# A hybrid encoder step on one NeuronCore: RWKV-7's triangular inverse on TensorE instead of GpSimd, and all queues in the order of a list scheduler

## The chip, the core and the metric

The kernel runs on one core of one Trainium2 chip. The metric is the device time of one execution in microseconds (us), the median of several runs. A core has TensorE (PE; its weight loads are shown as PEld), VectorE (DVE), ScalarE (ACT), GpSimd (POOL) and SyncE (SP, which here only issues DMA transfers). Each works through a queue of its own, in order; semaphores make one wait for another. The program fixes the order of every queue when it is built.

## The reference, cut to what matters

One inference step of a two-layer encoder trunk, in float32, for a prompt of 512 tokens and a sample of 32 tokens with states of its own. Layer 0: half SwiGLU, a mixer of RG-LRU and retention, cross-attention to a memory, half SwiGLU. Layer 1 the same with RWKV-7 as its mixer. Each part ends in `x = LayerNorm(ALPHA * x + part(x))`. The RWKV-7 recurrence, for each of 16 heads with 64 keys and 64 values, is

```
def step(S, inp):
    r_t, w_t, k_t, v_t, kk_t, b_t = inp
    sa = jnp.einsum('bhvk,bhk->bhv', S, -kk_t)
    S = S * w_t[:, :, None, :] + sa[..., None] * b_t[:, :, None, :] + v_t[..., None] * k_t[:, :, None, :]
    return S, jnp.einsum('bhvk,bhk->bhv', S, r_t)
...
s_last, o = lax.scan(step, s0.astype(f32), (tm(r), tm(decay), tm(k), tm(v), tm(kk), tm(kk * iclr)))
```

Done by chunks of 32 tokens it needs, for every chunk and head, the inverse of a triangular 32x32 matrix I + N with ones on the diagonal, where N (strictly triangular) holds the products of the chunk's keys among each other.

## The kernel before, in words

*The halves.* All 544 tokens lie as columns: half A has 256 columns, half B 288 (256 of the prompt and the sample's 32). Features lie on partitions. Two Python generators (`half_main`, one per half) walk through the eight stages of `STAGES`; a small task runner (`Kern.run`) switches between them and side tasks, and so decides in which order instructions are emitted.

*Products with weights.* `linear` takes a granule, a block of 128 columns of weights and up to 1024 rows: 512 KB, loaded by SyncE's queue to a buffer `wr`, split into a high and a low part in a slot `W` (ScalarE writes the high part, VectorE or GpSimd subtracts for the low part, `_split`), and multiplied in 24 matmuls of 128x128 by 256 or 288 columns: high by high, low by high, high by low. Usually both halves share a granule. Between layer 1's mixer and its end each half loads its own (`SOLO`), so that one half's products can fill the other's waits; half A may run ahead to the end there, but only behind its own recurrence.

*The recurrence (stage mix1).* `wkv` borrows three weight slots, one load buffer, two of the four PSUM banks of the products and three of the other four. It goes over nine blocks: four of 64 tokens of A, four of B and the sample's 32; a block has one or two chunks of 32 tokens. Five tasks run side by side, coupled by events:

- `wkv_prep` makes the decays, keys and rows of a block; its first instruction is a product on GpSimd (`K.gtt(a4, k, vb("k_k"))`, line 1807). For each chunk it multiplies the keys (KL) by the rows (X) into the masked 32x32 matrices, and writes N to DRAM (`dn`, line 1861). Event `kl` marks a chunk, `kb` the block.
- `wkv_solve` (lines 1873 to 1912) waits for `kb`. It loads N back with a head, chunk and quarter of the rows to a partition (tile P, line 1886), clears Z (in tile LC), and runs 31 steps of forward substitution on GpSimd, two operations each. Z goes to DRAM (`dz`) and from there in four loads into the corners of block-diagonal 128x128 matrices (`tb`, in a slot W; two buffers, so a block waits for the chain of the second block before it). Then it fires `prep`.
- `wkv_load` transposes keys and values for a chunk.
- `wkv_chain` is the recurrence itself, chunk after chunk: 16 products X by state (96 rows to 32 columns of the array), one eviction, four products with the inverse (128x128, line 1986), four evictions, 16 products that update the state, four VectorE operations, and 16 products for the output.
- `wkv_norm` norms a block's output and applies the gate.

*The order of the work.* Every instruction goes through `plan`, which asks `Clock.op` when it would run by an estimate (an engine's occupied times and its operands' times; tasks of a negative band, the recurrence among them, are planned as if other work were not there). The estimate becomes the instruction's priority (`cur_priority`, line 386), and the tile framework's own scheduler (`schedule_with_timeline_sim=True`, line 2083) puts the queues in order by these priorities and its own simulated times.

Of the kernel before, what the change touches and what calls it, by code (L numbers as in the profile page):

```python
# [3 lines left out]

# [42 lines left out]
MEM_FILL = 28  # L47
LOG_G = np.log1p(-(2.0 ** (-5.0 - np.arange(4, dtype=np.float32)))).astype(np.float32)
# [3 lines left out]
def const_arrays():  # L52
# [32 lines left out]
    c["wmask"] = m  # L85
    sg = np.ones((128, 1), np.float32)
# [16 lines left out]
class Res:  # L103
    """Things that are taken and given back, with the times from which they are free."""
# [27 lines left out]
class Line:  # L132
    """The spans of time in which an engine is taken; a later comer may fill a gap."""
# [28 lines left out]
class Clock:  # L162
    """An estimate of when instructions run, in ns: what an engine does and what its operands wait for.
    It orders the emission and the engines' queues, and nothing else rests on it."""
# [24 lines left out]
    def ready(self, outs, ins=()):  # L189
        """When the operands of a transfer are free and written."""  # L190
# [9 lines left out]
    def renew(self, old, new):  # L200
        """A tile takes over the room of an older one."""
        if old is not None and old.tensor.name in self.cells:
            c = self.area(new)[0]
            c[1] = self.cells.pop(old.tensor.name).max()
# [43 lines left out]

class Arena:
# [26 lines left out]
    def top(self, n):  # L276
        """The last n elements."""
# [50 lines left out]
class Arenas:  # L328
    """Several arenas as one."""
# [44 lines left out]
class Kern(Clock):  # L374
    def __init__(self, tc, ins, outs, consts, stages):
        super().__init__()
        self.tc, self.nc, self.i, self.o, self.c = tc, tc.nc, ins, outs, consts
# [6 lines left out]
    def plan(self, eng, dur, outs, ins, queue=None):  # L384
        s = self.op(eng, dur, outs, [t for t in ins if t is not None and not isinstance(t, (int, float))], self.band, queue)
        self.tc.cur_priority = 10000000 + int(s) + self.band * (BAND if self.band > 0 else 0000)

    def mm(self, out, lhsT, rhs, start=True, stop=True):
        n = free_size(rhs)
        if lhsT.dtype == F32R:  # L390
            cost = (n if n >= 256 else max(4 * n, 128)) / 2.4 + 2
        else:
            cost = 4 * (max(n, 62) / 2.4) + 2
        self.plan("pe", cost, [out], [lhsT, rhs])
        self.nc.tensor.matmul(out, lhsT, rhs, start=start, stop=stop)  # L395

    def tr(self, out, in_, k0=0):
        k = in_.shape[0]
        self.plan("pe", 109.0, [out], [in_])
        self.nc.tensor.transpose(out, in_, self.ident[k0:k0 + k, k0:k0 + k])  # L400

    def _v(self, out, ins, fast=False):
        fast = fast and all(t.space != PSUM for t in ins)
# [1684 lines left out]
```

## Time and profile before

| | |
|---|---|
| median of 3 runs | 3021.44 us (3020.57 to 3023.3) |
| span of the profiled execution | 3028.7 us |
| instructions | 54637 |
| PE / PEld / DVE / ACT / POOL busy | 2833.4 / 2716.3 / 1743.4 / 1276.8 / 830.1 us |
| HBM read | 313.09 MB, 108 GB/s over the span with the writes |
| mean granted TensorE clock | 0.945 |

The span is what the profiler saw between the first and the last instruction of one execution; nothing else of that execution's time is recorded. In the rows of the profile a name such as `mm<-XHB,W` means: PSUM tile mm written from tiles XHB and W; a line is that of a helper (395 is every matmul, 408 a VectorE product, 412 a GpSimd product, 486 a ScalarE activation, 491 a DMA), so one goes by tiles. A float32 matmul has two entries in the trace, a float32r matmul one. Busy time of PE counts every matmul from its start to its modelled end, so the tail of a lone matmul counts as busy. The granted clock is 1.00 at full speed.

### The profile page before, as it was taken

The page shows a single profiled execution, that of the slowest core. Times are in us where ns is not written, and L with a number is a line of the kernel's source. Part 1 is how long each engine was busy: PE and PEld are TensorE (multiplying, and loading weights), DVE is VectorE, ACT ScalarE, POOL GpSimd, SP SyncE. Part 2 cuts the span into 40 slices and gives each one's busy share as a digit, 9 for nine tenths or more (in the row PEclk, how much of TensorE's full clock was granted, in tenths as well). Part 3 has the DMA queues.
Part 4 walks back from the last instruction along what each step waited for, and adds up shares of the span by engine and source line. Part 5 has one row for each costly group of instructions (what it writes and reads, how often), then busy time and mean ns, then how long its engine had stood idle before and what let it go on. Part 6 is the DMA issues. An engine that isn't in the chain of part 4 may idle for free.

```text
span 3028.7 us, 54637 instructions
## 1 busy us (share of the span) xinstructions
PE 2833.4 (94%) x22456; PEld 2716.3 (90%) x22456; DVE 1743.4 (58%) x3099; ACT 1276.8 (42%) x2184; POOL 830.1 (27%) x1088
## 2 busy tenths in 40 slices
PE   9999998998999999999999898888878889999998
PEld 8999998998998999989999897776767779998997
DVE  5333337677767333365355756674675666767655
ACT  4223233665545222234244343343435455655544
POOL 2001104333313000032011212466375543422301
PEclk9999999999999999999999998788778879999999
DMA  6443443322332232322356453122223135645563
GB/s 182 126 119 115 130 119 97 88 68 81 98 98 84 85 90 84 89 87 77 90 155 179 120 168 106 39 65 62 69 73 87 49 98 174 177 141 157 169 176 93
DMA packets 626331, 330.56 MB, mean 109 GB/s; under 512 B 45480, under 2 KB 620160, under 8 KB 626080
## 3 DMA queue, kind: packets, MB, share of 16 engines
q1 hardware_dynamic: 617952, 317.06, 36.8%
q0 software_dynamic: 3488, 9.44, 1.0%
q8 instruction: 176, 2.88, 0.4%
q10 hardware_dynamic: 4640, 0.56, 0.1%
q14 instruction: 75, 0.61, 0.1%
HBM read 313.09 MB, written 13.92 MB: 108 GB/s over the span
## 4 chain that ended last, share of the span: by engine, by line
PE 66%; DVE 10%; POOL 9%; DMA 7%; ACT 5%; issue 3%; SPq 0%; ACTq 0%; DVEq 0%; POOLq 0%
PE mm L395 60%; PE ax L395 4%; POOL LC L412 3%; POOL P L412 3%; DMA P<-dn 3%; DVE W L408 2%; ACT arena L486 1%; ACT W L486 1%; DVE arena L408 1%; DMA wr<-in_ffn_up 1%; PE ax L400 1%; DVE arena L432 1%; POOL arena L412 1%; ACT L2049 1%; DVE XB L408 1%
## 5 line engine op out<-in xcount | busy, mean ns | idle before, releaser
L486 ACT ACTIVATE W<-wr 128x1024 fp32r<-128x1024 f32 (+1 forms) x558 | 577.0, 1038 | 737.4 <-PE mm L395 560.0
L408 DVE TENSOR_TENSOR W<-wr,W 128x1024 fp32r<-128x1024 f32 (+1 forms) x455 | 561.5, 1236 | 551.7 <-ACT W L486 542.8
L395 PE MATMUL mm<-XHB,W 128*128 128x288 f32 x3840 | 585.1, 302 | 14.1 <-ACT XHB L486 4.7
L395 PE MATMUL mm<-XHA,W 128*128 128x256 f32 x3840 | 538.4, 290 | 28.9 <-ACT XHA L486 11.6
L395 PEld LDWEIGHTS mm<-XHB,W 128*128 128x128 f32 x3840 | 532.4, 191 | 25.0 <-ACT XHB L486 5.8
L395 PEld LDWEIGHTS mm<-XHA,W 128*128 128x128 f32 x3840 | 499.7, 194 | 39.7 <-ACT XHA L486 16.0
L412 POOL TENSOR_TENSOR W<-wr,W 128x1024 fp32r<-128x1024 f32 (+1 forms) x103 | 251.0, 2439 | 606.2 <-ACT W L486 550.6
L395 PE MATMUL mm<-XLB,W 128*128 128x288 f32 x1984 | 318.7, 300 | 0.7 <-DVE XLB L408 0.7
L395 PE MATMUL mm<-HHB,W 128*128 128x288 f32 x1920 | 291.0, 301 | 11.4 <-ACT W L486 4.4
L395 PEld LDWEIGHTS mm<-XLB,W 128*128 128x128 f32 x1984 | 283.0, 190 | 3.2 <-DVE XLB L408 1.1
L395 PE MATMUL mm<-XLA,W 128*128 128x256 f32 x1984 | 284.7, 283 | 0.0
L395 PEld LDWEIGHTS mm<-HHB,W 128*128 128x128 f32 x1920 | 267.0, 191 | 15.0 <-ACT W L486 5.3
L395 PE MATMUL mm<-HHA,W 128*128 128x256 f32 x1920 | 265.7, 288 | 5.9 <-POOL W L412 2.2
L395 PEld LDWEIGHTS mm<-XLA,W 128*128 128x128 f32 x1984 | 259.1, 190 | 0.3 <-DVE XLA L408 0.2
L395 PEld LDWEIGHTS mm<-HHA,W 128*128 128x128 f32 x1920 | 247.1, 192 | 8.8 <-POOL W L412 2.6
L486 ACT ACTIVATE arena<-mm 128x256 f32<-128x256 f32 (+4 forms) x292 | 112.2, 387 | 305.1 <-PE mm L395 287.5
L432 DVE SCALAR_TENSOR_TENSOR arena<-mm,arena 128x288 f32<-128x288 f32 (+1 forms) x176 | 77.2, 439 | 157.7 <-PE mm L395 149.0
L395 PE MATMUL mm<-HLB,W 128*128 128x288 f32 x896 | 144.3, 301 | 0.3 <-DVE HLB L408 0.3
L412 POOL TENSOR_TENSOR P<-LC,P 128x66 f32<-128x66 f32 (+24 forms) x279 | 113.5, 407 | 84.6 <-DMA P<-dn 64.6
L395 PEld LDWEIGHTS mm<-HLB,W 128*128 128x128 f32 x896 | 130.1, 193 | 0.6 <-DVE HLB L408 0.5
L395 PE MATMUL mm<-HLA,W 128*128 128x256 f32 x896 | 129.3, 284 | 0.0
L412 POOL TENSOR_TENSOR LC<-LC,P 128x66 f32<-128x66 f32 (+24 forms) x279 | 115.0, 412 | 20.5
(426 smaller groups left out, 3612.0 us busy)
## 6 DMA issues: line engine op xcount, KB each, us to landing
wr<-in_ffn_up SPq DMA_DIRECT2D x246, 512.0 KB
wr<-in_ffn_down SPq DMA_DIRECT2D x96, 448.0 KB
wr<-in_l_w_rkv SPq DMA_DIRECT2D x48, 512.0 KB
wr<-in_ffn_down SPq DMA_DIRECT2D x40, 512.0 KB
wr<-in_l_w_in SPq DMA_DIRECT2D x24, 512.0 KB
wr<-in_l_w_out SPq DMA_DIRECT2D x24, 512.0 KB
wr<-in_xa_q SPq DMA_DIRECT2D x24, 512.0 KB
wr<-in_xa_o SPq DMA_DIRECT2D x24, 512.0 KB
```

Of the source, the lines that this page charges most:

```text
L395: self.nc.tensor.matmul(out, lhsT, rhs, start=start, stop=stop)
L400: self.nc.tensor.transpose(out, in_, self.ident[k0:k0 + k, k0:k0 + k])
L408: self.nc.vector.tensor_tensor(out, a, b, op=op)
L412: self.nc.gpsimd.tensor_tensor(out, a, b, op=op)
L432: self.nc.vector.scalar_tensor_tensor(out, a, s, b, op0=op0, op1=op1)
L486: return self.nc.scalar.activation(out, a, f, bias=bias, scale=scale, **kw)
L2049: nc.scalar.preload_act_table_set(name)
```

## The change

Two things change. First, `wkv_solve` computes the inverse on TensorE. For a chunk and group of four heads, four 32x32 matrices lie one below the other on 128 partitions; `product` multiplies them pairwise, each with a 32x32 corner of the array of its own (rows 32q, columns 32q). N comes straight from the keys and rows by 16 products per chunk, in both orientations. Masks (a new constant `winv` in tile LC) cut it into a block diagonal of 8x8 blocks and two bands outside; (I + D)^-1 of the diagonal comes from three doublings, and two steps widen it to 16 and to 32. There are no DRAM copies any more (`dn` and `dz` go), `tb` holds only the 32x32 matrices and has three buffers, and the chain's product by the inverse is 16 matmuls of 32x32 instead of 4 of 128x128. The evictions go to VectorE and ScalarE, one small sum to GpSimd. The solve's PSUM banks are those of the preparation. In the preparation the gates' products take one bank after the other instead of two at once, and seven products may go to GpSimd (`ett` instead of `tt`, and `f` for the first of two halves).

```
+    c["winv"] = np.tile(inv, (4, 1, 1))
...
     for b, (h, t0, L) in enumerate(w.blk):
         nch = L // 32
...
-        yield lambda: b < 2 or event(K, "chain", b - 2).set
...
-        for s in range(31):
-            nr, nt = s // 4 + 1, 31 - s
-            T = w.t[:, :nr * nt].rearrange("p (i t) -> p i t", i=nr)
-            K.gtt(T, Z[:, :nr, s:s + 1].to_broadcast([128, nr, nt]),
-                  N[:, s:s + 1, s + 1:].to_broadcast([128, nr, nt]))
-            K.gtt(Z[:, :nr, s + 1:], Z[:, :nr, s + 1:], T, ALU.subtract)
...
+        yield lambda: b < 3 or event(K, "chain", b - 3).set
...
+        def product(out, left, right):
+            for g in range(4 * nch):
+                for q in range(4):
+                    u = slice(32 * q, 32 * q + 32)
+                    K.mm(out[u, g], left[u, g], right[u, g], side=4)
...
+        ps, up, lo = yield from bank()
+        for c in range(nch):
+            X, KL = w.ck[b, c][:2]
+            for hd in range(16):
+                g, q = divmod(hd, 4)
+                u = slice(32 * q, 32 * q + 32)
+                K.mm(up[u, 4 * c + g], KL[0:64, hd, 32:64], X[0:64, hd, 32:64], side=4)
...
+        K.tt(dt, up, m(0))
+        K.tt(d, lo, m(1))
+        K.tt(et, up, m(2))
+        K.tt(ft, up, m(3))
+        w.ps.give(ps)
+        K.gtt(idt, dt, m(4), ALU.add)
+        yield
+        ps, p, pt = yield from bank()
+        product(p, dt, d)
+        product(pt, d, dt)
...
+        K.act(d2, both)
+        K.tt(id2, p, m(4), ALU.add)
...
+        product(p, d2[:, 1], d2[:, 0])
+        product(pt, id2, idt)
+        K.tt(id4, p, m(4), ALU.add)
+        K.act(gt, pt)
...
+        product(p, gt, id4)
+        product(pt, id4, gt)
...
+        K.act(t8, both)
...
+        product(p, et, t8[:, 0])
+        K.tt(iw, m(4), p, ALU.subtract)
...
+        product(p, t8[:, 1], iw)
+        product(pt, iw, t8[:, 1])
...
+        K.act(t16, both)
...
+        product(p, ft, t16[:, 0])
+        K.tt(iw2, m(4), p, ALU.subtract)
...
+        product(p, iw2, t16[:, 1])
+        K.act(cut(w.tb[b % 3]), p)
...
-            K.mm(pu[:, g * 64:g * 64 + 64], TB[:, 4 * c + g], RS[:, g])
+            for q in range(4):
+                u = slice(32 * q, 32 * q + 32)
+                K.mm(pu[u, g * 64:g * 64 + 64], TB[u, 4 * c + g], RS[u, g], side=4)
```

Second, the program is built twice. In the first pass a `Graph` notes every instruction with its engine, a price, its operands' dependencies and its planned start as a priority. `Graph.schedule` then runs a list scheduler over the whole graph: at each moment an engine takes, among the instructions whose operands are ready, the one with the earliest planned start. ScalarE may prefer one that needs no change of its function table (up to `SWAP` ns of priority), VectorE's operations on SBUF and GpSimd exclude each other, and transfers share one line. In the second pass `chain` ties each engine's instructions together in the order of these start times, and the framework's own simulation is off. The prices of `plan` change with it: a fixed 147 ns for VectorE in place of 70, 165 or 204 for ScalarE in place of 60 or 100, 190 + 2.1 ns per element for GpSimd in place of 150 + 2.0, n / 2.4 + 13 ns for a large product in place of n / 2.4 + 2, and small products count a half or a quarter where two or four share the array (`side`).

```
+            while f and f[0][0] <= t:
+                k = heappop(f)[1]
+                heappush(a, (prio[k], k))
+            p, k = heappop(a)
...
+            elif e == "dma":
+                issue = 700.0 if l == "g" else 50.0
+                free[l] = t + issue
...
+                dma = max(t + issue + 1300.0, dma) + d
+                end = dma + 900.0
...
+    def chain(self):
...
+        for _, k in sorted((t, k) for k, t in enumerate(self.starts)):
+            i = self.made[k]
+            if i.engine in last:
+                self.tc.add_manual_dep(i, last[i.engine].name, info, reason="schedule")
+            last[i.engine] = i
...
-    with tile.TileContext(nc, schedule_with_timeline_sim=True) as tc:
-        build(tc, ins, outs, consts, STAGES)
+            with tile.TileContext(nc, schedule_with_timeline_sim=False) as tc:
+                build(tc, ins, outs, consts, STAGES, graph, starts)
...
+    graph = Graph()
+    program_of(graph, None)
+    at = graph.schedule()
+    nc = program_of(None, [t for e, t in zip(graph.eng, at) if e != "x"])
```

More of the change, by code (lines that the diff above doesn't have):

```diff
@@ L200, in renew @@
     def renew(self, old, new):
+        if old is not None and self.graph is not None:
+            self.graph.renew(self, old, new)
         if old is not None and old.tensor.name in self.cells:
@@ L249 @@
+class Planned(Exception):
+    pass
 class Arena:
@@ L468, in bn @@
+        self.note(self.nc.vector.bn_stats(tmp, a))
         self._v(out, [tmp])
[L469 removed]
+        self.note(self.nc.vector.bn_aggr(out, tmp))
     def act(self, out, a, f=AF.Copy, bias=None, scale=1.0, accum=None):
[L472 to L477 removed]
@@ L478, in act @@
-        self.plan("a", dur, [out] if accum is None else [out, accum], [a])
+        dur = (165 if a.space == PSUM else 204) + free_size(out) / 1.2
+        dur += 88 * ((bias is not None and not isinstance(bias, float)) + (not isinstance(scale, float)))
+        self.plan("a", dur, [out] if accum is None else [out, accum], [a, bias, scale], sets=TABLES.get(f))
         kw = {}
@@ L696, in build @@
         K.run()
+        if starts is not None:
+            K.chain()
 VEC = {}
@@ L1814, in wkv_prep @@
         K.stt(a4, a4, -0.5, a3, ALU.mult, ALU.mult)
-        two = yield from w.pb.take(2)
-        for j in range(8):
-            for ps, q in zip(two, (0, 64)):
+        for q, t, nm in ((0, a1, "w0"), (64, a3, "a0")):
+            ps = yield from w.pb.take()
+            for j in range(8):
                 K.mm(ps[:, j * L:j * L + L], K.w2a2[q:q + 64, j * 128:j * 128 + 128], h.tw[q:q + 64, t0:t0 + L])
-        for ps, t, nm in zip(two, (a1, a3), ("w0", "a0")):
             K.tt(t, ps[:, :F].rearrange("p (a b) -> p a b", a=8), vb(nm), ALU.add)
@@ new lines, in bank @@
+        def bank():
+            ps = yield from w.ps.take()
+            return ps, cut(ps[:, :256]), cut(ps[:, 256:])
+        ps, up, lo = yield from bank()
[5 more added lines that the diff above has]
+                K.mm(up[u, 4 * c + g], KL[0:64, hd, 32:64], X[0:64, hd, 32:64], side=4)
+            for hd in range(16):
+                g, q = divmod(hd, 4)
+                u = slice(32 * q, 32 * q + 32)
+                K.mm(lo[u, 4 * c + g], X[0:64, hd, 32:64], KL[0:64, hd, 32:64], side=4)
@@ new lines, in wkv_solve @@
+        K.tt(dt, up, m(0))
[8 more added lines that the diff above has]
+        product(pt, d, dt)
+        both = ps.rearrange("p (s n) -> p s n", s=2)[:, :, :n].rearrange("p s (g t) -> p s g t", t=32)
+        K.act(d2, both)
+        K.tt(id2, p, m(4), ALU.add)
+        w.ps.give(ps)
+        yield
+        ps, p, pt = yield from bank()
@@ L1912, in wkv_solve @@
+        ps, p, pt = yield from bank()
+        product(p, iw2, t16[:, 1])
+        K.act(cut(w.tb[b % 3]), p)
+        w.ps.give(ps)
         event(K, "prep", b).fire(K)
+        yield
 def wkv_load(K, w):
```

340 lines of the change are left out of this document (240 added, 100 removed).

## The prediction

> **What bounds the kernel now.** I read the page's first two parts, then the table of stretches, then the chain of waits inside the stretch that stands out, then the tiles on that chain.
>
> ```profile
> span 3028.7 us, 54637 instructions
> ...
> PE 2833.4 (94%) x22456; PEld 2716.3 (90%) x22456; DVE 1743.4 (58%) x3099; ACT 1276.8 (42%) x2184; POOL 830.1 (27%) x1088
> ...
> PEclk9999999999999999999999998788778879999999
> ```
>
> TensorE carries the kernel: 94% busy over the span. But the clock line drops in one place, slices 25 to 33. I put stage borders there, beside one dense stretch as a yardstick:
>
> ```profile
> 0.00:1887.00 1887.00, 1809.44 (x13995) 1781.60 (x13996) 1003.20 (x1856) 739.55 (x1276) 360.74 (x332) 0.98 0.38 110
> 1887.00:2478.00 591.00, 498.76 (x4365) 421.05 (x4365) 391.68 (x729) 253.36 (x471) 333.40 (x669) 0.80 0.25 64
> 2478.00:3029.00 551.00, 525.17 (x4100) 513.61 (x4099) 348.52 (x515) 283.85 (x438) 135.91 (x87) 0.98 0.54 155
> ...
> 100.00:200.00 100.00, 100.00 (x804) 100.00 (x803) 37.14 (x54) 26.72 (x37) 8.54 (x13) 1.00 0.43 124
> ```
>
> The columns after the length are busy us and counts of PE, PEld, DVE, ACT, POOL, then clock, DMA share, GB/s. The middle stretch of 591 us is the RWKV recurrence. Its clock is 0.80, its instructions few: in the dense stretch a product takes 100/804 = 124 ns. Busy time there counts each product's tail of 0.2 to 0.3 us, so 498.76 flatters it. The useful part I count from the large products in that stretch:
>
> ```profile
> L395 PE MATMUL mm<-XHB,W 128*128 128x288 f32 x384 | 78.0, 344 | 4.7 <-ACT W L486 2.5 <-DVE W L408 2.2
> L395 PE MATMUL mm<-HHA,W 128*128 128x256 f32 x256 | 41.1, 311 | 5.7 <-POOL W L412 2.2 <-DVE XA L432 1.8 <-DVE W L408 1.7
> L395 PE MATMUL mm<-XLB,W 128*128 128x288 f32 x192 | 39.7, 332 | 0.0
> L395 PE MATMUL mm<-XHA,W 128*128 128x256 f32 x198 | 36.6, 338 | 15.9 <-POOL W L412 11.1 <-ACT XHA L486 4.9
> ...
> L395 PE MATMUL mm<-XLA,W 128*128 128x256 f32 x160 | 24.1, 292 | 0.0
> ...
> L395 PE MATMUL mm<-HLA,W 128*128 128x256 f32 x64 | 10.6, 306 | 0.0
> ```
>
> That is 384 + 256 + 192 + 198 + 160 + 64 = 1254 products with weights ("filler", work of the two halves outside the recurrence), at 124 ns 156 us. The other 4365 - 1254 = 3111 entries are the recurrence's own and some attention. Their price lies between 29 and 60 ns (fence of prices below), 90 to 187 us; I take 53 ns, 164 us, near the upper end, since many use the whole array. Useful work is thus 156 + 164 = 320 of 591 us, 54%. So 271 us of this stretch is waiting and half clock. What makes it wait stands in the chain of waits of this window:
>
> ```profile
> 1900.68 9.14 DMA P<-dn
> ...
> 1940.22 1.00 POOL arena L412
> ...
> 1955.03 0.71 DVE W L408
> 1955.76 3.57 DMA dn<-W
> 1959.40 11.23 DMA P<-dn
> ...
> 1994.30 1.00 POOL arena L412
> ...
> 2003.57 4.89 DMA dz<-LC
> ```
>
> In the waits in total, the tile dn and the costliest groups of the page, the same loop shows as:
>
> ```profile
> ACT arena L486 <- POOL arena L412: 67.3, 9, 17.6
> ...
> L491 SPq DMA_DIRECT2D P<-dn x12: 345/540/627, 1900.7 to 2439.8; - x12
> ...
> L412 POOL TENSOR_TENSOR P<-LC,P 128x66 f32<-128x66 f32 (+24 forms) x279 | 113.5, 407 | 84.6 <-DMA P<-dn 64.6
> ...
> L412 POOL TENSOR_TENSOR LC<-LC,P 128x66 f32<-128x66 f32 (+24 forms) x279 | 115.0, 412 | 20.5
> ```
>
> One block of 64 tokens goes round this loop: its N goes to DRAM (dn) and comes back in another layout (P<-dn, 9 to 11 us), GpSimd runs 31 pairs of small operations on it, and the inverse goes out (dz, 4.9 us) and in again. From 1959.40 to 2003.57 + 4.89 this is 49 us. GpSimd's part is (113.5 + 115.0) / 9 blocks = 25.4 us and more where VectorE is busy. Then the point that matters: the first step of preparing the *next* block (POOL arena, at 1940.22 and 1994.30) is queued on GpSimd behind the solve, and ScalarE waits for it (67.3 us, 9 times). From 1940.22 to 1955.76 that block is prepared, and its own round trip starts. Solve and preparation run one after the other, so the loads P<-dn of nine blocks are (2439.8 - 1900.7) / 8 = 67 us apart.
>
> **The change part by part.** *The solve leaves GpSimd and the DRAM round trips.* All 558 small GpSimd operations go (228.5 us), and with them the dn, P, dz and W<-dz transfers on SP's and ScalarE's queues and the two waits for them. Nothing is then queued in front of the next block's first step.
>
> *TensorE takes it over.* For a block of two chunks: 64 products that form N both ways, and 11 products of 32 matmuls each, together 416; for the sample's single chunk 208. That is 8 x 416 + 208 = 3536 matmuls. Each counts twice in the trace (18 matmuls with bones in the code, 36 entries), so 7072 entries. Prices:
>
> ```profile
> L395 PE MATMUL mm<-arena,bonest 128*128 128x512 f32 (+1 forms) x36 | 24.7, 804 | 7.4 <-ACT arena L486 7.4
> ...
> 1981.65 0.43 PE L395 MATMUL ax<-wr,XLA 96*32 96x64 f32 x16
> 1982.02 0.28 PE L400 MATMUL ax<-identt,VA 128*32 128x128 f32 x1
> ...
> 1986.12 1.00 PE L395 MATMUL ax<-arena,W 128*128 128x64 f32 x8
> 1987.05 0.71 PE L400 MATMUL ax<-identt,W 64*128 64x64 f32 x8
> ...
> 1997.38 1.13 PE L395 MATMUL ax<-XLA,wr 128*64 128x32 f32 x32
> 1998.43 2.08 PE L395 MATMUL mm<-XHA 64*64 64x64 f32 x32
> ...
> L395 PE MATMUL ax<-wr,XLA x64: 218/219/267, 1981.7 to 1997.2; 96*32 96x64 f32 x32, 64*64 64x64 f32 x32
> ```
>
> Four column tiles of 32: (0.43 - 0.22) / 15 = 14 ns per entry, or 0.37 / 16 = 23 with the change of shape behind it. Two tiles: (1.13 - 0.22) / 31 = 29. One place in the array only: (2.08 - 0.22) / 31 = 60, and 32 columns cost no less than 64. No trace here shows 32x32 tiles that differ in rows and columns at once. So the bounds are 14 and 60 ns: 99 and 424 us. Nothing below zero is possible, as none of it is on TensorE now. I take 16 ns, near the four-tile row, because a burst has 64 or 128 entries and pays the change of shape (0.15 us) once: 113 us. The Trainium skill's page "TensorE: Matmul & The Clock Gate" (section "Wait — 56ns, not 53.3ns?") states that starts never come closer than about 25 ns however short the product; that would be 177 us, 64 more, and the gain below would nearly vanish. The row with 14 disagrees with it for tiles side by side.
>
> *The chain's own product* by the inverse: 136 entries at (1987.05 - 1986.12) / 8 = 116 ns go, 15.8 us; 544 tile entries at 16 ns come, 8.7 us. With that the sum of PE work added is 113 - 7 = 106, say 110 us. That the gate products no longer alternate between two banks I cost at nothing: they run at 17.8 / 128 = 139 ns now, slower than one place alone.
>
> ```profile
> L395 PE MATMUL mm<-SUMB,LC 64*128 64x64 f32 x128 | 17.8, 328 | 0.0
> ...
> L408 DVE TENSOR_TENSOR XA<-XA,ax 128x256 f32<-128x256 f32 x64 | 21.9, 412 | 0.0
> ...
> L486 ACT ACTIVATE arena<-ax 128x512 f32<-128x512 f32 x12 | 6.9, 585 | 4.3 <-PE ax L395 4.3
> ```
>
> *Evictions:* 8 of VectorE per block at 0.41 us and 5 of ScalarE at up to 0.59 us: 30 and 26 us in all, against engines that are 391.68 and 253.36 busy of 591. Hidden; and GpSimd, 228 us lighter, takes more of the splits and of the products in the preparation that may now go to either engine.
>
> *How long the new solve takes.* Eight bursts, each waiting for the eviction before it. Alone: five of 128 entries, 1.8 + 0.22 + 0.59 = 2.6 us, and three of 64, 1.5 us: 18 us. Among other work: the chunk's chain has four such steps from 1981.65 to 1998.51, 4.2 us each, so 8 x 4.2 = 34 us. Two PSUM banks serve its 8 takes and the preparation's 8: at 2.5 us each 20 us a block, no limit. What is late next is the chain itself, 2 chunks x 16.9 = 34 us per block, in parallel with the solve of the next. I take 40 us a block for 67: 14 us to the first block, 8 x 40, and the 39 us behind the last load, 373; I use 400, because the second half's projections must still fit in.
>
> *Sum.* TensorE must place 164 + 110 = 274 us of the recurrence in those 400 us. At 80% useful (busy times clock gives 0.94 before the stretch and 0.93 behind it; the stretch itself has 0.54) it does 320, so 46 of filler; the other 156 - 46 = 110 us move behind the stretch, where the last row gives 525.17 x 0.98 / 551 = 0.93: 118 us. 400 + 118 = 518 for 591: a gain of 73. A period of 55 us instead of 40 changes this little (493 us hold 394 of work, 36 us move out: 532, gain 59), because TensorE is the bound then; the share of 80% decides. At 70%: gain 30. At 90%: 116.
>
> *The order of the queues* everywhere else: all engines now follow one simulated schedule with longer prices per instruction (0.147 us fixed for VectorE instead of 0.07) and with GpSimd and VectorE excluding each other.
>
> ```profile
> 500.00:600.00 100.00, 85.70 (x630) 83.01 (x629) 74.10 (x165) 58.23 (x109) 40.84 (x41) 0.93 0.29 85
> ...
> 1800.00:1900.00 100.00, 83.65 (x606) 77.74 (x606) 69.95 (x108) 39.48 (x68) 26.39 (x18) 0.87 0.39 107
> ...
> ACT W L486 <- DMA wr<-in_ffn_up: 77.2, 35, 5.9
> ```
>
> Outside the stretch TensorE is idle for 78 us before it (1887 - 1809.44) and 26 behind it, mostly where one half is normed (such as 500 to 600 and 1800 to 1900). A new order can win back part of 104 us or lose as much. I take -12. Total gain 85.
>
> The profiled span is 3028.7, 7 us above the median of the runs shown (3021.44); 3028.7 - 85 = 2944 in a profile, and 3021 - 85 = **2936 us** as the median.
>
> **The rivals.** *Queueing (20%).* The bursts of tiles are cut up by products with weights, the price per entry is the 23 ns that was seen with a change of shape behind it (+50 us of work), or the stretch reaches only 70%. For it: the 16-entry groups of the chunk at 1981.65 are cut by a transpose already. Gain 20 to 30 and none from the order: about 3000. The 25 ns of the page "TensorE: Matmul & The Clock Gate" of the Trainium skill would lead to about the same place.
>
> *No overlap of the tiles (7%, slower).* If the four products of a group, which lie on different rows and write different partitions of one PSUM bank, run one by one at 60 ns, the solve costs 2992 x 2 x 60 + 1088 x 16 = 376 instead of 113. Then the recurrence needs 164 + 370 = 534 us of TensorE, 600 us at 0.9, all filler moves out (156 / 0.93 = 168), and 768 stand against 591: about 3200. It decides from about 27 ns per entry on, where 73 x 0.93 = 68 us of work are added and the gain is gone. Against it: tiles on different columns do overlap here; for it: no row shows different rows. The Trainium skill's page "TensorEngine Tiling (Array Packing)" (section "Restrictions and Gotchas") says that different row tiles cannot access the same PSUM bank at the same time, which would be this case; no trace here shows it.
>
> *The order loses (8%, slower).* The schedule takes a weight load as done after 0.05 + 1.3 + 1.6 + 0.9 = 3.8 us (512 KB); ScalarE's waits for such loads are up to 5.9 us long, 77.2 us in 35 waits. Where it puts a split ahead of evictions on the faith of that, they wait behind it in ScalarE's queue, and TensorE for its banks. If that doubles the 104 us outside the stretch, 104 - 73 = 31 us are lost: about 3050. It decides from 73 us on. Against it: the plan's price of a load is nearly the same in both programs.
>
> *More than forecast (12%).* 90% in the stretch and half of the 104 us back: 116 + 52 = 168, about 2855. That the order does not reach the queues would only take the 12 us away.
>
> **How the numbers follow.** The forecast of 2936 has 53% (2890 to 2980, from 70 to 90% useful work), queueing 20%, more than forecast 12%, the two slower ones 15%. For 8 in 10 the range runs from 2855 to 3035: it leaves out most of the slower cases and the best of the fast one. Faster by over 0.2% (6 us, about what a measurement can tell from no change): 53 + 12 + most of 20 = 0.82; within: 0.03; slower: 0.15.
>
> **What would show it.** Right: no dn, dz or P tiles on any queue; GpSimd down by about 200 us; blocks some 40 us apart (by the first product of each block's solve); the stretch at about 400 us with a clock over 0.9; PE with 22456 + 7072 + 408 = 29936 entries; tile entries 14 to 16 ns apart in a burst. Wrong: tile entries 25 ns apart or more; a stretch over 500 us with PE under 90% busy; a table before 1887 with more idle time than 78 us.

## The result, and the profile after

| | before | changed |
|---|---|---|
| median | 3021.01 us (3018.6 to 3023.3, 4 runs) | 3124.07 us (3121.23 to 3125.74, 4 runs) |
| changed / before | | 1.0335, 95% interval 1.032 to 1.0349 |
| span of the profiled execution | 3028.7 us | 3121.6 us |

The kernel is 103 us slower where 85 us of gain were forecast. The first lines of the page of the changed kernel:

```profile
span 3121.6 us, 68986 instructions
PE 2934.0 (94%) x29936; PEld 2800.5 (90%) x29936; DVE 1755.8 (56%) x3116; ACT 1318.5 (42%) x2240; POOL 644.2 (21%) x548
PEclk9999999998999999999999997979997789999999
```

TensorE has exactly the 29936 entries of the forecast, and GpSimd 186 us less to do. The table of stretches with the borders of the prediction (PE, PEld, DVE, ACT, POOL busy us and counts, then granted clock, DMA share, GB/s):

```profile
0.00:1887.00 1887.00, 1802.36 (x13908) 1774.69 (x13908) 962.22 (x1812) 739.84 (x1261) 336.73 (x318) 0.98 0.37 108
1887.00:2478.00 591.00, 527.26 (x10038) 443.32 (x10036) 391.03 (x675) 248.60 (x461) 169.99 (x129) 0.83 0.19 55
2478.00:3122.00 644.00, 604.35 (x5996) 582.49 (x5995) 402.55 (x631) 330.03 (x518) 137.51 (x101) 0.95 0.47 136
```

Ahead of the recurrence 7 us more are idle (1887 - 1802.36 = 85 for 78). The stretch itself did not shrink to 400 us: at its old border 2478 TensorE still has 5996 entries to do instead of 4100, and everything behind is 93 us longer. The entries of the inverse, by form:

```profile
L579 PE MATMUL mm<-W 32*32 32x32 f32 x2720 | 34.9, 202 | 4.5 <-issue 3.2 <-DVE W L593 0.8 <-DVE arena L622 0.3
L579 PE MATMUL mm<-P,W 32*32 32x32 f32 x2176 | 31.5, 204 | 11.0 <-issue 7.5 <-ACT P L667 2.1 <-DVE W L593 1.3
...
L579 PE MATMUL mm<-W,P 32*32 32x32 f32 x544 | 7.3, 204 | 4.1 <-DVE W L593 4.1
L579 PE MATMUL mm<-P 32*32 32x32 f32 x544 | 7.2, 204 | 0.0
```

These are 5984 entries in 80.9 us, 13.5 ns each, tails included. In the timeline a burst looks so (start, length, count):

```profile
2001.60 1.29 PE L579 MATMUL mm<-W 32*32 32x32 f32 x128
...
2020.98 0.29 PE L579 MATMUL mm<-P,W 32*32 32x32 f32 x12
2022.91 0.63 PE L579 MATMUL mm<-P,W 32*32 32x32 f32 x50 [1.64 <-issue]
```

Less the 0.22 us of the last one's tail, 128 entries take 1.07 us, 8.4 ns each at full clock (granted 1.00 from 2001.6 to 2002.9). The prediction's rows had 29 and 60 ns for two places of the array and for one, so the four tiles on the array's diagonal run side by side, although they write one PSUM bank. The price was right, and the time was lost elsewhere. The last two lines show something new: one burst in two pieces, with a stop of 1.64 us between them in which TensorE waits for nothing but its own instructions (`issue`); more on it below.

Two markers for the recurrence: the scan that each block's preparation holds (first and last start of nine, then the start of the fourth, which is half A's last), and the store of the sample's state, which is the recurrence's end. Before:

```profile
L455 DVE TENSOR_TENSOR_SCAN arena<-LC,arena x9: 1207/1218/3009, 1872.9 to 2421.0; 128x512 f32<-128x512 f32 x8, 128x256 f32<-128x256 f32 x1
...
2030.61 1.21 DVE L455 TENSOR_TENSOR_SCAN arena<-LC,arena 128x512 f32<-128x512 f32 x1
...
L491 POOL DMA_DIRECT2D out_s_wkv<-arena x1: 885/885/885, 2522.0 to 2522.0; - x1
```

And in the changed kernel:

```profile
L640 DVE TENSOR_TENSOR_SCAN arena<-LC,arena x9: 685/1221/1349, 1887.0 to 2534.9; 128x512 f32<-128x512 f32 x8, 128x256 f32<-128x256 f32 x1
...
2084.34 1.22 DVE L640 TENSOR_TENSOR_SCAN arena<-LC,arena 128x512 f32<-128x512 f32 x1 [0.96 <-ACT arena L667]
...
L672 POOL DMA_DIRECT2D out_s_wkv<-arena x1: 885/885/885, 2611.6 to 2611.6; - x1
```

Blocks are (2534.9 - 1887.0) / 8 = 81 us apart; they were 68.5. These means hide two things. Within half A, (2084.34 - 1887.0) / 3 = 65.8 us lie between blocks, and (2030.61 - 1872.9) / 3 = 52.6 lay there before. From half A's last scan to half B's first it is 127 us and was 97: half B's preparation waits for its own projections. The recurrence ends 89.6 us later, and behind it the two kernels take nearly the same 507 and 510 us. That is nearly all of the 93 us by which the profiled executions differ.

### The profile page after: what moved, and what is told of

Its sections match the earlier page's. It is cut to its first block, busy times and chain, and to the rows that moved or that the text cites. A ratio compares the mean times of both kernels' runs of the same rounds, so it can differ in the third digit from the quotient of the medians.

```text
span 3121.6 us, 68986 instructions
## 1 busy us (share of the span) xinstructions
PE 2934.0 (94%) x29936; PEld 2800.5 (90%) x29936; DVE 1755.8 (56%) x3116; ACT 1318.5 (42%) x2240; POOL 644.2 (21%) x548
## 4 chain that ended last, share of the span: by engine, by line
PE 82%; DVE 5%; issue 4%; ACT 3%; DMA 3%; POOL 2%; POOLq 0%; ACTq 0%; SPq 0%; DVEq 0%
PE mm L579 73%; PE ax L579 7%; PE ax L584 2%; DVE W L593 1%; ACT W L667 1%; POOL W L597 1%; ACT arena L667 1%; DMA wr<-in_ffn_up 1%; DMA wr<-in_l_w_out 1%; DVE XA L593 1%; ACT L2286 0%; DVE arena L593 0%; DMA wr<-in_l_w_rkv 0%; DVE XB L593 0%; POOL XB L597 0%
## 5 line engine op out<-in xcount | busy, mean ns | idle before, releaser
L597 POOL TENSOR_TENSOR W<-wr,W 128x1024 fp32r<-128x1024 f32 (+1 forms) x102 | 243.1, 2385 | 858.3 <-ACT W L667 781.7
L667 ACT ACTIVATE arena<-mm 128x256 f32<-128x256 f32 (+5 forms) x295 | 114.1, 388 | 308.8 <-PE mm L579 294.8
L579 PEld LDWEIGHTS mm<-HLA,W 128*128 128x128 f32 x896 | 119.7, 194 | 0.4
L597 POOL TENSOR_TENSOR arena<-arena 128x256 f32<-128x256 f32 (+3 forms) x82 | 82.3, 1004 | 113.8 <-ACT arena L667 67.6
```

The lines of the kernel that those rows point to most:

```text
L579: self.note(self.nc.tensor.matmul(out, lhsT, rhs, start=start, stop=stop))
L597: self.note(self.nc.gpsimd.tensor_tensor(out, a, b, op=op))
L667: return self.note(self.nc.scalar.activation(out, a, f, bias=bias, scale=scale, **kw))
```

## The experiments

Ratios are to the kernel before, run beside each. The last column is the start of the store of the sample's state in the profiled execution, in us.

| kernel | median us | ratio, 95% interval | state stored |
|---|---|---|---|
| solve_alone | 3143.8 | 1.0404 (1.0386 to 1.0421) | 2625 |
| order_alone | 3107.1 | 1.0281 (1.0261 to 1.0302) | 2594 |
| solve_prices | 3126.7 | 1.034 (1.032 to 1.0361) | 2614 |
| solve_hold | 3126.2 | 1.0348 (1.0328 to 1.0368) | 2558 |
| changed_hold | 3123.6 | 1.0337 (1.032 to 1.0355) | 2578 |
| no_inverse_hold | 3029.0 | 1.003 (1.0011 to 1.0048) | 2495 |
| twice_hold | 3251.1 | 1.0767 (1.0744 to 1.0791) | 2670 |
| slow_solve | 3136.5 | 1.0371 (1.0351 to 1.0391) | 2629 |
| long_prep | 3177.5 | 1.0506 (1.0489 to 1.0524) | 2659 |
| before_first_step | 3060.4 | 1.0118 (1.0097 to 1.0139) | 2552 |
| before_hold | 3021.1 | 1.0001 (0.9985 to 1.0017) | 2527 |
| loose_tiles | 3213.5 | 1.0611 (1.0572 to 1.065) | 2679 |
| loose_tiles_x5 | 3897.8 | 1.2901 (1.2861 to 1.2942) | 3354 |
| loose_large | 3088.2 | 1.0219 (1.0194 to 1.0244) | 2539 |
| prices_alone | 3039.8 | 1.0058 (1.0041 to 1.0074) | 2530 |
| before_defer | 3047.8 | 1.0088 (1.0064 to 1.0112) | 2510 |

### The two parts by themselves

solve_alone is the kernel before with the new `wkv`, `wkv_prep`, `wkv_solve`, `wkv_chain` and the constant; scheduler and prices stay. order_alone is the changed kernel with these functions as before. solve_prices is the changed kernel with the queues put in order by the framework's simulation:

```
-    graph = Graph()
-    program_of(graph, None)
-    at = graph.schedule()
-    nc = program_of(None, [t for e, t in zip(graph.eng, at) if e != "x"])
+    nc = program_of(None, None)
```

> The kernel before with the new solve, preparation and chain product alone; prices and the framework's order of the queues are those of before. In the changed kernel half B's last granules of layer 1's first SwiGLU end at 1925 us instead of 1875, its projections for the recurrence at 2265 instead of 2155, and its recurrence starts at 2295 instead of 2174: about the 93 us that the span is longer. Theory 'solve': the 7072 tile entries and the lower clock beside half A's recurrence starve half B's projections; then this kernel is slower too, 3080 to 3120 us. Theory 'order': the list schedule lets half B fall behind; then this kernel is not slower, 2970 to 3020 us, and half B's projections end by about 2160.

> The changed kernel with the old solve on GpSimd, its preparation and its chain product: the new prices and the list schedule alone. Theory 'solve': near the kernel before, 3000 to 3040 us. Theory 'order': near the changed kernel, 3090 to 3130 us, with half B's projections ending after 2240. If both parts cost alone and add up, this and the solve alone lie each some 50 us above the kernel before.

> The changed kernel with the framework's own scheduler instead of the list schedule: new solve and new prices, no noted program. If the list schedule itself does the harm, this is at or below the kernel before, 2970 to 3020 us; if the prices that make the planned starts do it, it is near the changed kernel, 3090 to 3130; theory 'solve' expects 3080 to 3120 here as well.

Each part loses by itself: the solve 122 us, the order 86. They don't add up: together they cost 103. With the new solve already there, the new prices take 17 us away (3143.8 to 3126.7) and the list scheduler makes no measurable difference (3126.7 without it, 3124.1 with it). With the new prices and the list scheduler already there, the solve adds only 17 us (3107.1 to 3124.1). So what a part costs depends on which one is there first, and why they overlap by some 105 us stays open. The next sections take the solve apart, in the order and with the prices of before; no run leaves the inverse out of the changed kernel itself.

### Why half B's projections wait in solve_alone: held buffers

In solve_alone a hole stands out, in which TensorE is short of weights. The stretch 2130 to 2200 of solve_alone:

```profile
2130.00:2200.00 70.00, 47.00 (x805) 38.74 (x804) 40.68 (x70) 22.45 (x44) 18.50 (x16) 0.56 0.08 24
```

Only 24 GB/s are loaded. Rows of SyncE's queue in solve_alone, with loads of half A's output projection (`in_l_w_out`) ahead of the hole and the last and the next load of half B's projections (`in_l_w_rkv`) around it:

```profile
2099.85 7.78 SPq L496 DMA_DIRECT2D wr<-in_l_w_out  x2
2129.00 0.37 SPq L496 DMA_DIRECT2D wr<-in_l_w_rkv  x1
...
2202.58 0.37 SPq L496 DMA_DIRECT2D wr<-in_l_w_rkv  x1
```

The queue had loaded half A's output projection into buffers whose contents can't be used before A's norm, and half B's projections got nothing for 73 us. solve_hold tests whether the one causes the other; it lets half A's loads wait:

```
     yield event(K, "wkv", h.name)
+    if not isb:
+        yield event(K, "proj", "B")
     unlimit(h.solo)
```

> The new solve with the scheduler and prices of before, and half A's output projection may load its weights only when half B's projections are through. Theory 'held buffers' (A's early out-projection weights keep the lent weight buffers while B's projections wait for theirs, and B's path sets the end): B's last projection product moves from 2276 to 2210 us or earlier, and the time falls from 3144 to 3085 us or less. Theory 'TensorE load' (99 us of tile entries simply displace B's projections): the projections end within 20 us of 2276 and the time stays at 3130 to 3150. Theory 'preparation' (the blocks' preparation sets their period of 66 us): the period stays between 60 and 70 us in either case.

> The changed kernel with the same hold. Theory 'held buffers': 3060 to 3090 us, from 3124. Theory 'TensorE load': 3110 to 3135.

> The kernel before with the hold on half A's output projection alone. It loads those weights only after 2140 us as it is: within 10 us of the kernel before by the theory of held buffers.

The same stretch in solve_hold:

```profile
2130.00:2200.00 70.00, 56.38 (x948) 49.07 (x946) 42.20 (x66) 28.74 (x52) 15.07 (x11) 0.82 0.28 84
```

The hole is filled, the recurrence ends 67 us sooner (2625 to 2558), and the time falls by 18 us only. In the changed kernel the end of the recurrence comes 33 us sooner (2612 to 2578) for nothing. The held buffers are real and explain 18 of 122 us; the price of 60 that was expected for them fell. The kernel before doesn't suffer from them (before_hold). What is more, in these two pairs an earlier end of the recurrence brought little or nothing.

### No inverse, the inverse, and the inverse twice

no_inverse_hold leaves the 11 products and their evictions out (the 1088 entries that form N stay); twice_hold issues each product twice.

```
-        K.tt(dt, up, m(0))
...
-        K.act(cut(w.tb[b % 3]), p)
+        K.tt(cut(w.tb[b % 3]), up, m(2))
```

> As solve_hold, but the inverse is left out: the masked N is written in its place, so the 11 products a block, 5984 tile entries, and their evictions are missing. Theory 'the solve was the bound of the recurrence' (the prediction's): blocks 45 us apart or less and 2940 us or less. Theory 'preparation': blocks still 58 us apart or more. Theory 'TensorE load': the 5984 entries at 14 ns, 84 us, come off nearly whole, 60 to 85 us below solve_hold, whatever the period is. Without it: 25 us below at most.

> As solve_hold, with each of the 11 products a block issued twice over the same places, 5984 more tile entries of 14 ns, 84 us of TensorE work and 8 bursts a block that are longer. Theory 'TensorE load': 60 to 90 us above solve_hold. Theory 'preparation': 25 us above at most, since the solve lies beside the preparation of the next block.

The inverse costs 3126 - 3029 = 97 us, and a second one 125 more. Both are more than the 81 us that its entries occupy TensorE, and more than the 60 to 85 and 60 to 90 that were expected. That is the plainest result of the study: the inverse is paid in full. What of that is TensorE's time and what its evictions is not separated by these two; the next two sections narrow it down. And the kernel without any inverse is not faster than the one before, which did it on GpSimd. The scans (all nine, then the fourth) and what is left behind 2478 in no_inverse_hold:

```profile
L460 DVE TENSOR_TENSOR_SCAN arena<-LC,arena x9: 692/1217/1225, 1874.3 to 2401.4; 128x512 f32<-128x512 f32 x8, 128x256 f32<-128x256 f32 x1
...
2040.85 1.22 DVE L460 TENSOR_TENSOR_SCAN arena<-LC,arena 128x512 f32<-128x512 f32 x1
```

```profile
2478.00:3300.00 822.00, 518.07 (x4023) 507.87 (x4019) 358.16 (x507) 277.27 (x428) 140.24 (x88) 0.99 0.36 103
```

Its blocks are (2401.4 - 1874.3) / 8 = 66 us apart, against 68.5 with GpSimd's solve; in half A alone (2040.85 - 1874.3) / 3 = 55.5 against 52.6, so not closer at all. At 2478 it has 4023 entries left against 4100: 77 entries, some 10 us. As far as this comparison shows, GpSimd's 25 us per block and the two round trips through DRAM were beside other work all along.

### The solve made longer, the preparation made longer

Two kernels put idle GpSimd products by one into solve_hold, with no work for TensorE: slow_solve into the solve's chain, long_prep into the preparation's.

```
+        def slow(t):
+            for _ in range(3):
+                K.gtt(t, t, K.smask[:, 1:2].to_broadcast([128, free_size(t)]))
...
         K.act(d2, both)
+        slow(w.z2[0])
```

> As solve_hold, with 21 GpSimd products by one in the solve of each block, in place on d2, gt, t8, iw, t16, iw2 and tb: by the planner's prices 18.5 us longer from the first product to the inverse, no TensorE work more. Theory 'TensorE's work' (what the new solve costs is the time its tile entries take on TensorE): within 20 us of solve_hold's 3126. Theory 'the solve is a link of the chain that sets the end': 5 blocks of the second half times 18.5, 90 us more. The prediction's picture of a loop of 67 us would have said 9 x 18.5, 165 us.

> As solve_hold, with 16 GpSimd products by one in the preparation of each block, in place on a4, a1, a2 and a3: by the planner's prices 18.8 us longer, no TensorE work more, and the same GpSimd work as in the kernel with the slow solve. Theory 'preparation sets the period': blocks some 19 us further apart, 75 to 95 us above solve_hold. If it is only TensorE's work that counts: within 20 us.

In slow_solve the added products are (nearly all of) these rows, in long_prep the first row of the second fence:

```profile
L417 POOL TENSOR_TENSOR P<-P,LC 128x512 f32<-128x512 f32 x81 | 91.3, 1127 | 80.1 <-ACT P L491 76.5
L417 POOL TENSOR_TENSOR W<-W,LC 128x256 f32<-128x256 f32 x107 | 79.8, 746 | 170.1 <-DVE W L413 85.3 <-ACT W L491 80.3
```

```profile
L417 POOL TENSOR_TENSOR arena<-arena,LC 128x512 f32<-128x512 f32 x128 | 149.0, 1177 | 77.0 <-ACT arena L491 67.2 <-DVE arena L413 6.8
```

That is (91.3 + 79.8) / 9 = 19.0 us a block for the solve and 149.0 / 8 = 18.6 for the preparation. The scan of the fourth block tells what each did to half A's period. First solve_hold, then slow_solve, then long_prep:

```profile
2057.70 1.22 DVE L460 TENSOR_TENSOR_SCAN arena<-LC,arena 128x512 f32<-128x512 f32 x1 [0.18 <-ACT arena L491]
```

```profile
2060.26 1.23 DVE L460 TENSOR_TENSOR_SCAN arena<-LC,arena 128x512 f32<-128x512 f32 x1
```

```profile
2125.68 2.05 DVE L460 TENSOR_TENSOR_SCAN arena<-LC,arena 128x512 f32<-128x512 f32 x1 [1.33 <-POOL arena L417]
```

The first scans are at 1876.0, 1873.9 and 1887.8, so half A's blocks are 60.6, 62.1 and 79.3 us apart. The longer preparation goes into the period one to one (+18.7), the longer solve hardly at all (+1.5). So the preparation sets half A's period, and the solve lies beside the next block's preparation. The time of the whole: +51 us for the preparation, of some 150 put in and of 75 to 95 expected, and +10 for the solve. So the whole time does not hang on the period alone. In slow_solve the recurrence ends 71 us later (2629 for 2558), most of it behind the last block's scan (2492.2 for 2475.0), probably because no preparation is left there to hide the solve; and yet 10 us is all it costs.

### What any work on TensorE costs there

Three kernels add idle work to no_inverse_hold, at the solve's place, from constants, read by nobody and with no eviction: the 5984 tile entries of the inverse in one burst a block, five times as many, or 204 large float32 products.

```
+        ps, p, pt = yield from bank()
+        one = cut(K.smask)
+        for k in range(11):
+            product((p, pt)[k % 2], one, one)
+        w.ps.give(ps)
```

```
+        for k in range(12 * nch):
+            K.mm(ps[:, 256 * (k % 2):256 * (k % 2) + 256], K.bones, K.smask[:, :256])
```

> As the kernel without the inverse, with its 11 products a block (5984 tile entries) put back as idle work: one burst a block into one bank, from a constant, read by nobody, with no eviction. What it lacks against solve_hold is the chain of eight products and evictions, what it has is the occupancy. Theory 'occupancy' (any TensorE time in this stretch is paid in full): 84 us of entries at 14 ns, 70 to 100 us above the kernel without the inverse (3029). Theory 'chain' (the price of 97 us comes from the dependent steps and their evictions): 40 us above at most. The prediction's view of the stretch, idle time that takes up more work: 20 us at most.

> The same with five times the entries (29920, a burst of 3520 a block, some 49 us at 14 ns). It shows the price of an entry in a long stretch of nothing else and the clock that is granted there. If tiles run at full clock: 14 ns an entry, 419 us in all. Theory 'tiles lower the clock' (granted clock of 0.74 to 0.78 where they are thick): the clock in such a burst falls to 0.8 or less and an entry takes 17 ns or more.

> As the kernel without the inverse, with 24 large float32 products a block (128x128 by 256 columns, some 0.43 us each, 87 us in all) in place of the tiles, read by nobody. Theory 'occupancy': the same price as for the tiles, 70 to 100 us above 3029. If the price is one of small tiles (their clock, their bursts): 40 us above at most.

The large products, one burst of 42 entries among them, in loose_large:

```profile
2107.57 9.23 PE L400 MATMUL mm<-LC,bonest 128*128 128x256 f32 x42
```

An entry takes (9.23 - 0.22) / 42 = 215 ns, 408 of them 87.5 us, and the kernel is 59 us slower (3088.2 - 3029.0): with no chain and no eviction, two thirds of plain TensorE time are paid. The loose tiles cost 184 us, twice the inverse itself, with the same number of entries and no chain. So the chain of eight products is not what makes the tiles dear; longer bursts are worse. The timeline of one burst of loose_tiles_x5 shows why:

```profile
2601.44 2.35 PE L400 MATMUL mm<-LC 32*32 32x32 f32 x257
2606.14 1.27 PE L400 MATMUL mm<-LC 32*32 32x32 f32 x128 [2.35 <-issue]
2609.90 1.93 PE L400 MATMUL mm<-LC 32*32 32x32 f32 x128 [2.49 <-issue]
...
2617.13 1.93 PE L400 MATMUL mm<-LC 32*32 32x32 f32 x128 [1.55 <-issue]
2620.61 1.93 PE L400 MATMUL mm<-LC 32*32 32x32 f32 x128 [1.55 <-issue]
2624.09 1.93 PE L400 MATMUL mm<-LC 32*32 32x32 f32 x128 [1.55 <-issue]
```

After a first piece every 128 entries are followed by a stop, and a round takes 2624.09 - 2620.61 = 3.48 us, 27 ns an entry, although 128 entries take 1.93 us at half clock (granted 0.50 there) and 1.27 at full clock (the second line, granted 1.00). The round that began at full clock was no shorter, 2609.90 - 2606.14 = 3.76 us, so it is not the array's speed that sets it. "Issue" is time in which TensorE waits for nothing that the profile shows. The queue that carries instructions tells what it is; packets and MB in no_inverse_hold, loose_tiles and loose_tiles_x5:

```profile
q8 instruction: 188, 3.08, 0.4%
```

```profile
q8 instruction: 234, 3.83, 0.5%
```

```profile
q8 instruction: 421, 6.90, 0.8%
```

29920 entries more bring 233 packets and 3.82 MB more: 128 entries and 16.4 KB a packet, 128 bytes an entry (a weight load and a matmul). The stops come about once per packet. The tiles' rows in loose_tiles_x5 and loose_tiles (busy, then idle before them), and TensorE's waits for its own issue in loose_tiles_x5 and loose_large (us, times, longest):

```profile
L400 PE MATMUL mm<-LC 32*32 32x32 f32 x29920 | 457.4, 233 | 383.1 <-issue 383.1
L400 PE MATMUL mm<-LC 32*32 32x32 f32 x5984 | 96.0, 217 | 49.5 <-issue 49.5
```

```profile
PE mm L400 <- issue: 383.1, 212, 3.8
PE mm L400 <- issue: 0.5, 1, 0.5
```

There are 212 stops for 233 packets, and 457.4 + 383.1 = 840.5 us of the 869 that loose_tiles_x5 costs. So a long run of tiles goes as fast as its instructions are brought in, one packet in 3.5 us, and not as fast as the array. In loose_tiles the same sum is 145.5 of 184 us; the rest is not accounted for. The Trainium skill's page "Runtime: NRT & Kernel Launch" (section "Instruction fetch mechanics") says that instructions come in blocks of 16 KiB, 256 instructions, and that the cost of crossing from block to block is mostly hidden. The size agrees with the packets here; that it is hidden holds for the large products (0.5 us in all of loose_large) and not for these. The stop was at hand in the changed kernel too, but small. Waits of TensorE for its own issue in the changed kernel:

```profile
PE mm L579 <- issue: 12.5, 15, 1.8
...
PE ax L579 <- issue: 1.5, 2, 0.8
```

In solve_hold and twice_hold:

```profile
PE mm L400 <- issue: 6.3, 6, 1.8
...
PE ax L400 <- issue: 1.1, 2, 0.7
```

```profile
PE mm L400 <- issue: 65.2, 45, 2.7
...
PE ax L400 <- issue: 4.0, 5, 1.6
```

7 us of the 97 that the inverse costs go to it, but 62 us of the next 125, where bursts hold 128 to 256 entries. The granted clock falls where the stops are. The table of stretches of loose_tiles_x5 from 2605 to 2650 has 0.54 (behind the burst, from 2700 to 2740, it is 0.50):

```profile
2605.00:2650.00 45.00, 22.68 (x1552) 21.09 (x1556) 2.42 (x8) 0.00 (x0) 0.00 (x0) 0.54 0.04 12
```

### The order of the queues

prices_alone is order_alone with the framework's simulation in place of the list scheduler (the edit of solve_prices).

> The kernel before (old solve, framework's simulation for the queues) with the new prices of plan alone, so that it differs from the kernel with the order alone (3107) by the list scheduler only. Theory 'the new prices give a worse order of emission': 3090 to 3125 us. Theory 'the list scheduler gives the worse queues': 3020 to 3040 us.

The new prices cost 18 us, so 67 of the 86 us come from the list scheduler. One place can be named. The table of stretches from 1900 to 2000, in the kernel before and in order_alone:

```profile
1900.00:2000.00 100.00, 91.08 (x699) 76.12 (x698) 68.38 (x137) 42.55 (x75) 60.74 (x126) 0.81 0.19 48
```

```profile
1900.00:2000.00 100.00, 63.47 (x443) 47.99 (x444) 67.54 (x132) 33.85 (x59) 54.51 (x118) 0.68 0.16 43
```

Half A's recurrence has begun there, and 28 us more of TensorE's time stand empty. Its two longest waits there in order_alone are for VectorE's part of a split of weights and for ScalarE's `XB`, a tile of half B:

```profile
PE mm L579 <- DVE W L628: 12.5, 3, 10.0
PE ax L579 <- ACT XB L667: 10.4, 1, 10.4
```

But prices_alone has nearly the same hole (70.28 us busy) and loses only 18, so the hole is not all of it. What else the list scheduler loses with the old solve stays open.

### Two attempts to mend the kernel before

before_first_step moves the first product of a preparation to VectorE, away from behind GpSimd's solve. before_defer puts the last four operations of a preparation off into the next one, ahead of its scan; a block's output products and its norm must then wait for them.

```
-        K.gtt(a4, k, vb("k_k"))
+        K.tt(a4, k, vb("k_k"))
```

```
-        K.tt(a2, r, k)
-        K.tt(a2, a2, vb("r_k"))
...
+        if last is not None:
+            yield from bonus(*last)
         yield
         K.scan(flat(a2), K.smask[:, :F], flat(a1), 0.0)
```

> The kernel before with one operation moved: the first product of a block's preparation runs on VectorE instead of on GpSimd, where it stood behind the solve of the block ahead. The prediction's reading (solve and preparation run one after the other because of this queue): blocks 10 us closer or more, 40 us faster or more. Theory 'preparation sets the period, and the solve lies beside it': within 12 us of the kernel before, since the preparation is only begun earlier by the 7.5 us of a wait.

> The kernel before with the last four operations of a block's preparation (the bonus of the rows and keys) put off into the next block's preparation, ahead of its scan, where VectorE waits for ScalarE's gates; for the last block of each half they stay. 5 us or so come off the steps from one block to the next. Theory 'preparation sets the period' with the price that 19 us more had (51 us): 10 to 15 us faster, 3005 to 3015. If only TensorE's work counts: within 6 us of the kernel before. If it disturbs the planner as the moved first step did: 20 to 40 us slower.

Both lose, 38 and 27 us. In before_defer the recurrence does end 12.5 us earlier, as a shorter preparation should bring; then 532 us follow behind it instead of 507. In before_first_step it ends 30 us later, and 508 follow. The first also gives VectorE nine more operations, and the second adds waits, so it is not shown that the order alone does it; but two edits as small as these move the time by 38 and 27 us. That is the yardstick for the differences above: of no_inverse_hold's 7 us, solve_prices' 3, slow_solve's 10 or the 18 of the held buffers and of the prices, nothing should be made, and the 59 of loose_large and the 51 of long_prep are rough. The direction of the main result does not hang on them: the inverse, its doubling, and three kernels with idle TensorE work all came out slower by 59 to 869 us. No kernel of the study beats the one before.

## Why the prediction was wrong, step by step

**TensorE bounds the kernel: right. That 271 of its 591 us there were room: wrong.** loose_large is the direct test: 87.5 us of plain products with no dependence cost 59. The 320 us of useful work were also too low by the prediction's own rows. It took 53 ns for each of 3111 entries, between bounds of 29 and 60, but `mm<-SUMB,LC` has 128 entries in 17.8 us, `ax<-arena,W` 128 at 116 ns, and one more row of that stretch reads

```profile
L395 PE MATMUL mm<-arena,bonest 128*128 128x512 f32 x30 | 22.1, 853 | 7.4 <-ACT arena L486 7.4
```

These 286 entries take some 55 us where the sum has 15, an estimate that makes the room 40 us smaller by itself.

**The loop: wrong, and this is the step that failed.** "Solve and preparation run one after the other" and "I take 40 us a block for 67". The evidence was a wait of ScalarE for GpSimd in front of each preparation and a chain of waits that went through the solve. Half of it was misread: "from 1940.22 to 1955.76 that block is prepared" takes the first step of one block and the end of another for one preparation. The first steps of half A's second to fourth blocks, not quoted then, show it:

```profile
L412 POOL TENSOR_TENSOR arena<-HLA,pv x3: 1041/1044/1274, 1885.2 to 1994.3; 128x512 f32<-128x512 f32 x3
```

The block whose N goes out at 1955.76 had begun at 1885.2 and had its scan at 1921; the one that begins at 1940.22 has its scan at 1979. Each preparation is a row of some 30 dependent steps, and the solve of the block ahead lies beside it. The 67 us were no single loop's time either: they are a mean over half A, where scans are 52.6 us apart, the step of 97 us to half B, and half B. The runs put in the loop's place: in half A the period is the preparation's own (long_prep 18.7 of 18.6 us, slow_solve 1.5 of 19); leaving the inverse out altogether leaves it at 55.5 there and at 66 over all blocks, where 40 was forecast. The wait in front of the first step is real, and taking it away (before_first_step) brought nothing.

**The price of a tile entry: right.** 13.5 ns measured for 16 forecast, 80.9 us for 5984 entries. The Trainium skill's page "TensorEngine Tiling (Array Packing)" (section "Restrictions and Gotchas") says that different row tiles cannot access the same PSUM bank simultaneously; the 8.4 ns at full clock, of tiles that write one bank, do not agree with it.

**110 us of new work, of which 46 us of filler and more find room in a shorter stretch: wrong as a consequence.** As the loop didn't shorten, there was no gain to pay from. The work was then paid at its price and above: 97 us for 81. The forecast's gain of 73 is 110 us of added work and 183 us less waiting; the first term held (97 for the inverse alone), the second is about 0 (no_inverse_hold against before, within the 27 to 38 us by which a small edit moves this kernel).

**GpSimd: right and of no use.** It lost 186 us of work, and even the kernel without any inverse gained nothing from that. That the evictions are hidden was not tested by itself.

**The order, -12: neither borne out nor refuted.** By itself it costs 86 us, of it 18 from the prices; that would be the sign of the rival "The order loses", whose mechanism (loads taken as done too early) was not tested. On top of the new solve, which is where the forecast put it, it takes 20 us away (3143.8 to 3124.1), nearly all of it the prices; that has the sign of the forecast and is within what a small edit moves, so the agreement may be luck.

**The rivals.** "No overlap" fell. "Queueing" saw bursts cut up and a dearer entry, but kept a gain from the loop. The case that came true, that the solve was hidden and TensorE's price is paid for nothing, was not among them, though it is the second of the plain questions to ask of any work that is moved: who waits for it now?

What decides the last 500 us is not settled. Behind the store of the state ten kernels take 505 to 516 us, whatever their total; there the end of the recurrence seems to set the time, as in the kernel before and the changed one. The others take 532 to 580. That in these TensorE's remaining work sets the end is argued from the two groups, not shown.

## What to carry to other kernels

A step on the chain of waits is not yet a step that sets the period: lengthen it by a known amount, with idle work on an engine that has room, and see how much of it comes out at the end. Here 19 us a block came out of half A's period as 1.5 in the solve and 18.7 in the preparation, and of the whole time as 10 and 51 us in all. Such a run on the kernel before, ahead of the change, would have tested the loop on which the forecast rested. A mean distance between blocks should be taken within one regime: 67 us was a mean over two halves and the gap between them. Idle time of a bound engine between dependent steps is not room for more work until a run shows it; here plain work put there was paid to two thirds and the moved inverse to more than its whole price.

## What was not expected of the hardware

Long runs of small matmuls are bound by the supply of instructions: one packet of 16.4 KB (128 float32 entries, each a weight load and a matmul) in 3.5 us, 27 ns an entry, where the array itself does four diagonal 32x32 tiles at 8.4 ns an entry. Bursts of 64 and 128 entries with other work between them meet it seldom (17 stops, 14 us, in the changed kernel), runs of 700 meet it often: loose_tiles has 25 stops in its nine bursts, 49.5 us, and pays 184 us for the same entries for which solve_hold pays 97. The granted clock is low with the stops (0.54 in the middle of such a run) and still 0.50 in the 40 us behind it, so that what comes behind starts slow.
